# A hybrid decoder block on one core: sums of retention's results by heads, attention's first values split around the exponentials, next weights within the cover steps

## The chip, the core and the metric

The kernel runs on one core of a Trainium2 chip. The core has a matrix engine (TensorE, PE in the profile; its weight loads are PEld), VectorE (DVE), ScalarE (ACT), GpSimd (POOL) and SyncE (SP), which here only issues transfers. Each engine works through its own list of instructions in order, and an instruction waits for what it needs from the others. Sixteen DMA engines move data between the chip's main memory and the on-chip memory, or within main memory; a transfer is issued by SP or by GpSimd, in the order of that engine's list. The metric is the device time of one execution in microseconds (us), lower is better.

## The reference

The block takes 1024 tokens of width 1024 and computes, in float32:

```python
h = modulate(rms_norm(x, g1), sh1, sc1)              # shift and scale from the conditioning vector
parts = split(h @ w_in)                              # retention q, k, v, gate; attention q, k, v of 3 groups; 2 gates
ro = retention(rotary(rq), rotary(rk) / 16, rv)      # 4 heads, chunks of 128 tokens, state 256 x 512
ro = group_norm(ro) * gn_g + gn_b
ret_out = (silu(rg) * ro) @ w_ret_out                # 2048 -> 1024
for g in 3 groups:                                   # 4 heads each, dilation 1, 4, 16
    o[g], lse[g] = dilated_attention(q[g], k[g], v[g], bias[g])
att = sum over g of softmax(lse)[g] * o[g]
merged = sigmoid(gate_a) * ret_out + sigmoid(gate_b) * (att @ w_att_out)
x = x + g1 * (merged @ w_o)
x = x + g2 * (relu(modulate(rms_norm(x)) @ w_ff1) ** 2 @ w_ff2)
out = rms_norm(x, gf)
```

## The kernel before

Every matrix product is made of three passes (`mm3`, lines 201 to 205): each operand is split into a high part, a rounded copy made by ScalarE, and a low part, the rest, made by a subtraction on VectorE. So each weight tile costs a copy on ScalarE and a subtraction on VectorE before TensorE may use it (`split_w`, lines 191 and 192). Large products are cut into 2 by 2 blocks and use seven block products instead of eight, for which sums of blocks are needed.

The work is a list of steps (`Steps`). A step has weight loads, which SP issues into a ring of three raw tiles (line 85), and a body, which writes out instructions. Before the body of an ordinary step runs, the next two steps' weights are split, if raw tiles and split tiles are there. A step marked manual gets a function instead (`ahead`, or the first argument of its body) and calls it where it wants the next step's weights split. The order in which bodies write their instructions is the order on each engine; nothing is reordered later.

The stages, with their places in the profiled execution: the first norm and the attention values (to about 160 us), queries and keys of retention and attention with the weight sums by DMA (to about 560), values of retention, retention (about 660 to 985), attention keys, scores and values for the first pair of heads (to about 1150) and for the second (to about 1296), the output projections, and the MLP.

**Retention.** Four heads of eight chunks. Each chunk (`chunk`) has state matmuls, scores, and between them the projection of retention's gate. GpSimd makes in each chunk the low part j of a later chunk's queries and keys (line 613) and one power for the norm, gr (line 728), which VectorE uses in its next instruction (line 729). In the first four chunks of the following head, `u_final` finishes a head's result, a quarter at a time, and SP stores it to the main-memory tensor y (line 670); the last head is finished in attention's first step.

**Sums of results.** The output projection of retention needs four sums of the blocks of y: t1 = b11 + b12, t3 = b12 + b22, t2 = t1 + b22, t4 = t2 + b21. They are made by DMAs within main memory that GpSimd issues (`result_sums`, `dma_sum`, lines 563 and 564): a copy, then a transfer that adds into its destination, 2 MB each over all four heads, eight in all. They are issued in attention's first step, after the last head's result is stored, each waiting on GpSimd for the one before. Their readers are loads of the output projection, after 1300 us.

**Attention.** For each pair of heads six steps (`att_step`) project keys and compute the scores of the step before. Then come cover steps (`cover_step`): each projects one tile of the merge gates, so that TensorE has work while softmax and the products with the values go on. For the first pair there are four (n = 0 to 3), for the second three, and `gate_step` is its fourth. Their contents:

- n = 0: the scores of the last combination; `scores_end` (maxima, line 1254; exponentials in place with their sums, line 1266), `weights` (the merge weights of the three groups, lines 1336 to 1347, with one exponential on ScalarE at line 1340), `pscale` of group 0 (probabilities times weights, VectorE line 1361 and ScalarE line 1363).
- n = 1: only the gate tile; in its middle `v_split` makes the high (vh, ScalarE, line 1295) and low (vl, VectorE, line 1296) parts of group 0's values.
- n = 2: products of group 0's probabilities with the values (`pv`), woven with the gate matmuls; the split of group 1's values.
- n = 3, or the gate step: products of group 1 (and 2), and `pscale` of group 2 after the fourth k block of the gate matmuls.

In `pv`, TensorE transposes blocks of probabilities (line 1378), ScalarE and VectorE split the transposed block (pth, ptl, lines 1382 and 1383), and TensorE multiplies (lines 1402 to 1404). At the end of a head the result is added up on VectorE (line 1415), which frees the accumulator for the next. The values are loaded by SP (`v_fetch`, line 1289), group 0's in the last of the six steps.

Of the kernel before, what the change touches and what calls it, by code (L numbers as in the profile page):

```python
# [17 lines left out]
P = 128  # L18
# [116 lines left out]
def block_kernel(ctx, tc, io, stop=None, dbg=None):  # L135
# [3 lines left out]
    def fv(t):  # L139
        return t.bitcast(F32)  # L140
# [382 lines left out]

    y_d = dram.tile([P, 4, 8, 512], F32, name="y")
    yt_d = {n: dram.tile([P, 8, 512], F32, name=f"y{n}") for n in ("t1", "t2", "t3", "t4")}
    YB = ("11", "12", "21", "22")

    WN = ("11", "12", "22", "s1", "s2", "s3", "s4")  # L530
# [26 lines left out]
        nc.gpsimd.dma_start(s4, s2)  # L557
        add(s4, src[1, j])

    def dma_sum(out, x, y):  # L560

        flat = lambda t: t.rearrange("p a b -> p (a b)").rearrange("p (a b) -> p a b", b=2048)
        nc.gpsimd.dma_start(flat(out), flat(x))
        nc.gpsimd.dma_start(flat(out), flat(y), accum_op=ALU.add, max_dma_last_dim=8192)
# [6 lines left out]
    def result_sums():  # L571
        b11, b12, b21, b22 = (y_d[:, i] for i in range(4))
        dma_sum(yt_d["t1"], b11, b12)
        dma_sum(yt_d["t3"], b12, b22)
        dma_sum(yt_d["t2"], yt_d["t1"], b22)
        dma_sum(yt_d["t4"], yt_d["t2"], b21)

    hd = {}
# [23 lines left out]
    def flat(ps):  # L602
        return ps.rearrange("p a b -> p (a b)")
# [56 lines left out]
    def u_final(h, es=range(4)):  # L660
        for e in es:
            i = h * 4 + e
            t = hd["on", h][e]
            for hf in range(2):
                neg = 16 if hf == i % 2 else 0
                b = t[:, 512 * hf:512 * hf + 512]
                nc.scalar.activation(b, b, AF.Identity, scale=gnv[0][:, neg + i:neg + i + 1],
                                     bias=gnv[1][:, neg + i:neg + i + 1])
            nc.vector.tensor_mul(t, t, hd["srg", h, e])
            nc.sync.dma_start(y_d[:, 2 * (i % 2):2 * (i % 2) + 2, i // 2], t.rearrange("p (t x) -> p t x", t=2))  # L670

    def chunk(h, c, ahead, w=None):
        p = R["p"]
# [61 lines left out]
            nc.scalar.activation(hd["srg", h, c // 2], flat(hd["rgp"]), AF.Silu)  # L735
        if h > 0 and c < 4:
            u_final(h - 1, (c,))

    def wsplit(ap):
        return ap, split_w  # L740
# [547 lines left out]
            lo = A["l", g, j] = v_tile(pair, g, j, "vl")  # L1288
            nc.sync.dma_start(fv(lo).rearrange("p (a b) -> p a b", a=4), v_rows(pair, g, j))

    def v_split(pair, g):
        for j in range(2):
            lo = A["l", g, j]
            hi = v_tile(pair, g, j, "vh")
            nc.scalar.copy(hi, fv(lo))
            nc.vector.tensor_sub(lo, fv(lo), fv(hi))
            A["v", g, j] = (hi, lo)

    def vblk(g, blk, a, i):
        j, b = (blk % 2, blk // 2) if g == 1 else (blk // 4, blk % 4)  # L1300
# [26 lines left out]
    def weights(pair):  # L1327

        p, st = A["p"], A["st"]
        stn = [st[:, 0], A["stn"][:, 1], A["stn"][:, 2]]  # L1330
        mx = p.tile([P, 8, 2], F32, tag="mx", name=f"mx{pair}")
        wt = p.tile([P, 3, 8, 2], F32, tag="wt", name=f"wt{pair}")
        pr = p.tile([P, 3, 8, 2], F32, tag="pr", name=f"pr{pair}")
        sm = p.tile([P, 8, 2], F32, tag="ssum", name=f"ssum{pair}")
        wg = p.tile([P, 2, 8, 2], F32, tag="wg", name=f"wg{pair}")
        nc.vector.tensor_max(mx, stn[0][:, :, 0:2], stn[1][:, :, 0:2])
        nc.vector.tensor_max(mx, mx, stn[2][:, :, 0:2])
        for g in range(3):
            nc.vector.tensor_sub(wt[:, g], stn[g][:, :, 0:2], mx)
        nc.scalar.activation(wt, wt, AF.Exp)  # L1340
        for g in range(3):
            nc.vector.tensor_mul(pr[:, g], wt[:, g], stn[g][:, :, 2:4])
# [123 lines left out]
    def att_step(pair, i):  # L1466

        g, a = combos[i]

        def body(*args):  # L1470
            ps = ps_mm(f"ak{pair}{i}")
            gen = proj_gen(ps, args[-1])
            if i == len(combos) - 1:
                v_fetch(pair, 0)
            if i > 0:
                last = combos[i - 1]
                weave(gen, NK, scores_gen(pair, *last), len(SB[last[0]]), lag=2)
            elif pair == 0:
                args[0](1, True)
                for _ in range(4):  # L1480
                    next(gen)
                on_T(H - 1, NC - 1)
                drain(gen)
                u_final(H - 1)
                result_sums()
                open_att()
                args[0](3)
            else:

                weave_pv(at(gen, 0, lambda: v_split(0, 2)), NK - 1, 0, 2)  # L1490
            if i == 0:
                A["st"] = A["p"].tile([P, 3, 8, 4], F32, tag="st", name=f"st{pair}")
                bias_load(pair)
            k_split(pair, g, a, ps)
            if i > 0:
                scores_end(pair, *last)
                if last[1] == 1:
                    stats_out(pair, last[0])
        return body

    def cover_step(pair, n):
# [34 lines left out]
    for pair in range(2):  # L1536
# [14 lines left out]
    def gate_step(w):  # L1551
# [72 lines left out]
    def r_x_load(i):  # L1624

        n, c = RSEQ[i]
        b = RPLAN[n][0]
        src = y_d[:, YB.index(b)] if b in YB else yt_d[b]
        for m in range(4):
            Q["x", i, m] = mh(f"rl{i}{m}")  # L1630
            nc.sync.dma_start(fv(Q["x", i, m]), src[:, 4 * c + m])

    def r_x(i, j):

# [818 lines left out]
```

## Time and profile before

| | us |
|---|---|
| median of 3 runs | 2242.24 (2241.17 to 2242.70) |
| the profiled execution | 2241.44 |
| its span, first to last instruction | 2239.7 |
| TensorE busy | 2183.1 (97%) |
| VectorE busy | 1456.5 (65%) |
| ScalarE busy | 908.5 (41%) |
| GpSimd busy | 145.9 (7%) |

The TensorE clock granted was 0.995 of full speed over the span. The times of one engine's rows are its own; a row that says "x3" merges three like instructions in a row. A bracket behind a row gives the engine's idle time before it and what ended it. A wait for several events is put down to the one that came last. The profile's ends of matmuls are modelled: consecutive matmuls overlap, so a matmul's row may be longer than the distance to the next.

### The profile page before, as it was taken

How to read it: one execution, taken by the hardware profiler on the slowest of the kernel's cores; microseconds unless marked ns; L12 is line 12 of the kernel's file. 1: busy time of each engine (PE TensorE's matmuls, PEld its weight loads, DVE VectorE, ACT ScalarE, POOL GpSimd, SP SyncE). 2: the span in 40 equal slices, each digit the busy share in tenths (PEclk: the TensorE clock that was granted, in tenths of full speed). 3: DMA queues.
4: the chain of work that ended last, by engine and by line, in shares of the span. 5: the costliest groups of instructions: out<-in, count | busy, mean ns of one | idle time of the engine just before them, and what ended most of it. 6: DMA issues, size and time to landing. Idle time of an engine off the chain costs nothing.

```text
span 2239.7 us, 27138 instructions
## 1 busy us (share of the span) xinstructions
PE 2183.1 (97%) x10130; PEld 1805.4 (81%) x10130; DVE 1456.5 (65%) x2285; ACT 908.5 (41%) x1665; POOL 145.9 (7%) x168
## 2 busy tenths in 40 slices
PE   7999999999999999999999999999999999999998
PEld 5887888888887888888888788888777777888887
DVE  6527777764548778855555654677866665787845
ACT  4332332223334445544634634524444444533412
POOL 0001110000012122200000000001000000000003
PEclk9999999999999999999999999999999999999999
DMA  9538999634775556559723365654243343745322
GB/s 362 198 142 263 295 286 291 188 113 174 240 272 188 169 182 202 191 171 238 225 73 98 91 225 178 244 182 148 75 151 139 139 155 150 269 144 169 122 85 76
DMA packets 154371, 408.93 MB, mean 183 GB/s; under 512 B 27062, under 2 KB 54973, under 8 KB 149822
## 3 DMA queue, kind: packets, MB, share of 16 engines
q1 hardware_dynamic: 148542, 363.14, 46.4%
q0 software_dynamic: 5696, 44.04, 8.2%
q8 instruction: 80, 1.31, 0.2%
q14 instruction: 53, 0.43, 0.1%
HBM read 316.27 MB, written 156.13 MB: 211 GB/s over the span
## 4 chain that ended last, share of the span: by engine, by line
PE 81%; DVE 9%; ACT 4%; DMA 4%; issue 2%; POOL 0%; SPq 0%; POOLq 0%; DVEq 0%; ACTq 0%
PE qap L201 5%; PE qap L205 5%; PE qap L203 5%; PE av L763 4%; PE rg L203 2%; PE rg L201 2%; PE rg L205 2%; PE fp L201 2%; PE fp L203 2%; PE fp L205 2%; PE ak L201 2%; PE f2a L203 2%; PE f2a L205 2%; PE f2a L201 2%; PE ak L203 2%
## 5 line engine op out<-in xcount | busy, mean ns | idle before, releaser
L201 PE MATMUL qap<-hh,qaw 128*128 128x512 f32 x216 | 85.1, 394 | 4.7 <-DVE qat L285 4.7
L203 PE MATMUL qap<-hl,qaw 128*128 128x512 f32 x216 | 85.0, 393 | 0.0
L205 PE MATMUL qap<-hh,qaw 128*128 128x512 f32 x216 | 85.0, 393 | 0.0
L613 POOL TENSOR_TENSOR j<-qk,j 128x512 fp32r<-128x512 f32 x32 | 43.8, 1369 | 460.0 <-ACT j L612 460.0
L1912 ACT ACTIVATE a<-a 128x512 f32<-128x512 f32 x48 | 30.3, 632 | 84.9 <-DVE a L1911 84.9
L258 DVE TENSOR_TENSOR qaw<-wa,qaw 128x512 fp32r<-128x512 f32 x54 | 37.0, 686 | 36.4 <-ACT qaw L248 36.4
L1266 ACT ACTIVATE P<-P,ng 128x128 f32<-128x128 f32 (+1 forms) x96 | 41.9, 438 | 39.2 <-DVE ng L1263 39.2
L258 DVE TENSOR_TENSOR fw<-w1r,fw 128x512 fp32r<-128x512 f32 x48 | 33.0, 688 | 37.5 <-ACT fw L248 37.5
L1809 POOL TENSOR_TENSOR accnf<-accnf,sqnf 128x256 f32<-128x256 f32 (+1 forms) x18 | 16.6, 921 | 624.3 <-ACT sqnf L1808 624.3
L2096 ACT CAST w2h<-w2s 128x512 fp32r<-128x512 f32 x36 | 22.4, 622 | 79.1 <-DVE w2s L2134 76.1
L201 PEld LDWEIGHTS qap<-hh,qaw 128*128 128x128 f32 x216 | 41.1, 190 | 13.6 <-issue 5.1
L201 PE MATMUL fp<-h2h,fw 128*128 128x512 f32 x128 | 50.0, 390 | 0.0
L203 PE MATMUL fp<-h2l,fw 128*128 128x512 f32 x128 | 49.8, 389 | 0.0
L201 PE MATMUL roa<-rh,rwl 128*128 128x512 f32 x128 | 49.8, 389 | 0.0
L203 PE MATMUL roa<-rl,rwh 128*128 128x512 f32 x128 | 49.8, 389 | 0.0
L205 PE MATMUL roa<-rh,rwh 128*128 128x512 f32 x128 | 49.8, 389 | 0.0
L205 PE MATMUL fp<-h2h,fw 128*128 128x512 f32 x128 | 49.8, 389 | 0.0
L1647 DVE TENSOR_TENSOR rwl<-rwl,rwh 128x1024 fp32r<-128x1024 f32 x25 | 30.2, 1221 | 29.0 <-ACT rwh L1677 29.0
L205 PEld LDWEIGHTS qap<-hh,qaw 128*128 128x128 f32 x216 | 41.1, 190 | 8.7
L203 PEld LDWEIGHTS qap<-hl,qaw 128*128 128x128 f32 x216 | 41.1, 190 | 8.5
L635 ACT COPY sm<-sT 128x128 f32<-128x128 f32 x32 | 8.5, 265 | 94.3 <-PE sT L626 94.3
L1809 POOL TENSOR_TENSOR accn<-accn,sqn 128x512 f32<-128x512 f32 x12 | 15.5, 1294 | 478.4 <-ACT sqn L1808 478.4
(3081 smaller groups left out, 7186.1 us busy)
## 6 DMA issues: line engine op xcount, KB each, us to landing
v<-vd SPq DMA_DIRECT2D x32, 512.0 KB, 5.5
raw<-in_w_ada_dram SPq DMA_DIRECT2D x32, 512.0 KB, 5.0
w1r<-in_w_ff_dram SPq DMA_DIRECT2D x32, 512.0 KB, 5.1
vd<-vo SPq DMA_DIRECT2D x24, 512.0 KB, 6.4
yt<-y POOLq DMA_DIRECT2D x6, 2048.0 KB, 15.3
xsd<-as SPq DMA_DIRECT2D x24, 512.0 KB, 2.7
w2r<-in_w_ff2s_dram SPq DMA_DIRECT2D x24, 512.0 KB, 7.6
em<-in_w_ada_dram SPq DMA_DIRECT2D x16, 512.0 KB, 10.2
```

The source lines that it names most:

```text
L201: nc.tensor.matmul(o, wl, xh, start=first, stop=False, skip_group_check=skip)
L203: nc.tensor.matmul(o, wh, xl, start=False, stop=False, skip_group_check=skip)
L205: nc.tensor.matmul(o, wh, xh, start=False, stop=last, skip_group_check=skip)
L258: nc.vector.tensor_sub(t[:, 512:], src, fv(t[:, :512]))
L613: nc.gpsimd.tensor_sub(t[:, 1], src, fv(t[:, 0]))
L635: nc.scalar.copy(sm, ps[:, :C])
L763: nc.tensor.matmul(av[g][c], x[k][:, c * C:(c + 1) * C], w[j][:, ws], start=k == 0 and (x, j) == parts[0], stop=k == NK - 1 and (x, j) == ...
L1266: nc.scalar.activation(v, v, AF.Exp, bias=ng[:, blk:blk + 1], accum_out=st[:, g, blk, 2 + a:3 + a])
L1647: nc.vector.tensor_sub(lo, fv(lo), fv(hi))
L1809: (nc.vector if f == 7 else nc.gpsimd).tensor_add(G["acc", key], G["acc", key], sq)
L1912: nc.scalar.activation(o, o, AF.Relu)
L2096: nc.scalar.copy(hi, src)
```

## The change

It has three parts.

1. **Sums by heads.** y and the four sum tensors become one tensor per head. A head's eight transfers (four copies, four adds, 512 KB each) are put on a list after the fourth chunk of the following head; each chunk ends with issuing one from the list (`result_sum`). The chunks from the thirteenth on issue one each, 20 in all; the remaining 12, four of the third head and eight of the last, are issued in attention's first step, where the eight large ones were.
2. **First values around the exponentials.** The high parts of group 0's values are made in cover step 0, after the gate tile's matmuls and ahead of `scores_end`; the low parts in `weights`, behind the exponential. Cover step 1 is left with the gate tile alone.
3. **Next weights within the step.** Cover step 3 and the gate step become manual. They split the next step's weights after the fourth k block, just ahead of `pscale` of group 2, instead of the next two steps' weights ahead of everything. The second of these splits is made ahead of the body of the step behind.

TensorE's list of instructions is unchanged.

```diff
-    y_d = dram.tile([P, 4, 8, 512], F32, name="y")
+    y_d = [dram.tile([P, 4, 2, 512], F32, name=f"y{h}") for h in range(H)]
...
+    def sums_of(h):
+        b11, b12, b21, b22 = (y_d[h][:, i] for i in range(4))
+        t1, t2, t3, t4 = (yt_d[n][h] for n in ("t1", "t2", "t3", "t4"))
+        return [(t1, b11, 0), (t1, b12, 1), (t2, t1, 0), (t2, b22, 1), (t4, t2, 0), (t4, b21, 1), (t3, b12, 0),
+                (t3, b22, 1)]
+
+    def result_sum():
+
+        if hd["sums"]:
+            out, x, add = hd["sums"].pop(0)
+            out, x = (t.rearrange("p a b -> p (a b)") for t in (out, x))
+            if add:
+                nc.gpsimd.dma_start(out, x, accum_op=ALU.add, max_dma_last_dim=8192)
+            else:
+                nc.gpsimd.dma_start(out, x)
...
         if h > 0 and c < 4:
             u_final(h - 1, (c,))
+        result_sum()
+        if h > 0 and c == 3:
+            hd["sums"] += sums_of(h - 1)
...
-    def v_split(pair, g):
+    def v_split(pair, g, low=True):
         for j in range(2):
             lo = A["l", g, j]
             hi = v_tile(pair, g, j, "vh")
             nc.scalar.copy(hi, fv(lo))
-            nc.vector.tensor_sub(lo, fv(lo), fv(hi))
             A["v", g, j] = (hi, lo)
+            if low:
+                v_low_part(g, j)
...
         nc.scalar.activation(wt, wt, AF.Exp)
+
+        for j in range(2):
+            v_low_part(0, j)
...
-                result_sums()
+                hd["sums"] += sums_of(H - 1)
+                while hd["sums"]:
+                    result_sum()
...
                 drain(gen)
+                v_split(pair, 0, False)
                 scores_end(pair, *combos[-1])
                 weights(pair)
...
             elif n == 1:
-                drain(at(gen, 4, lambda: v_split(pair, 0)))
+                drain(gen)
...
-                weave_pv(at(gen, 3, lambda: [pscale(2, a) for a in range(2)]), NK - 1, pair, 1)
+
+                gen = at(gen, 3, lambda: (args[0](2), [pscale(2, a) for a in range(2)]))
+                weave_pv(gen, NK - 1, pair, 1)
...
-            steps.add(cover_step(pair, n), more + [wsplit(io["w_gate"][len(COVER[0]) * pair + n])], manual=n == 2)
+            steps.add(cover_step(pair, n), more + [wsplit(io["w_gate"][len(COVER[0]) * pair + n])], manual=n > 1)
...
-        gen = at(gen, 3, lambda: [pscale(2, a) for a in range(2)])
+        gen = at(gen, 3, lambda: (ahead(2), [pscale(2, a) for a in range(2)]))
...
-    steps.add(gate_step, [wsplit(io["w_gate"][len(COVER[0] + COVER[1])])])
+    steps.add(gate_step, [wsplit(io["w_gate"][len(COVER[0] + COVER[1])])], manual=True)
```

More of the change, by code (lines that the diff above doesn't have):

```diff
@@ L522, in etile @@
         return R["p"].tile([P, 1024], dt, tag="E", bufs=12, name=name)
-    y_d = dram.tile([P, 4, 8, 512], F32, name="y")
-    yt_d = {n: dram.tile([P, 8, 512], F32, name=f"y{n}") for n in ("t1", "t2", "t3", "t4")}
+    y_d = [dram.tile([P, 4, 2, 512], F32, name=f"y{h}") for h in range(H)]
+    yt_d = {n: [dram.tile([P, 2, 512], F32, name=f"y{n}{h}") for h in range(H)] for n in ("t1", "t2", "t3", "t4")}
     YB = ("11", "12", "21", "22")
@@ L558, in quarter_sums @@
         add(s4, src[1, j])
[L560 to L564, printed above, removed]
     def gn_signs():
@@ L569, in gn_signs @@
             nc.vector.tensor_scalar_mul(gnv[i][:, 16:], vec[:, v:v + 16], -1.0)
[L571 to L578, printed above, removed]
+    def sums_of(h):
[11 more added lines that the diff above has]
+                nc.gpsimd.dma_start(out, x)
+    hd = {"sums": []}
     NG = H * NC
@@ L669, in u_final @@
             nc.vector.tensor_mul(t, t, hd["srg", h, e])
-            nc.sync.dma_start(y_d[:, 2 * (i % 2):2 * (i % 2) + 2, i // 2], t.rearrange("p (t x) -> p t x", t=2))
+            nc.sync.dma_start(y_d[h][:, 2 * (i % 2):2 * (i % 2) + 2, e // 2], t.rearrange("p (t x) -> p t x", t=2))
     def chunk(h, c, ahead, w=None):
@@ L1295, in v_split, with v_low_part @@
             nc.scalar.copy(hi, fv(lo))
-            nc.vector.tensor_sub(lo, fv(lo), fv(hi))
             A["v", g, j] = (hi, lo)
+            if low:
+                v_low_part(g, j)
+    def v_low_part(g, j):
+        hi, lo = A["v", g, j]
+        nc.vector.tensor_sub(lo, fv(lo), fv(hi))
     def vblk(g, blk, a, i):
@@ L1549, in block_kernel, with gate_step @@
     mh_ctx = ExitStack()
-    def gate_step(w):
+    def gate_step(ahead, w):
         ps = ps_mm("gate9")
         gen = at(proj_gen(ps, w), 2, lambda: v_split(1, 2))
-        gen = at(gen, 3, lambda: [pscale(2, a) for a in range(2)])
+        gen = at(gen, 3, lambda: (ahead(2), [pscale(2, a) for a in range(2)]))
         weave_pv(gen, NK - 1, 1, 1, 2)
@@ L1627, in r_x_load @@
         b = RPLAN[n][0]
-        src = y_d[:, YB.index(b)] if b in YB else yt_d[b]
         for m in range(4):
+            h = 2 * c + m // 2
+            src = y_d[h][:, YB.index(b)] if b in YB else yt_d[b][h]
             Q["x", i, m] = mh(f"rl{i}{m}")
-            nc.sync.dma_start(fv(Q["x", i, m]), src[:, 4 * c + m])
+            nc.sync.dma_start(fv(Q["x", i, m]), src[:, m % 2])
     def r_x(i, j):
```

## The prediction

> **What bounds the kernel now.** I read the page first (busy time by engine), then the busy time by stage, then who waited for whom on TensorE, and last the three engines' rows in order of time around each of these waits.
>
> ```profile
> span 2239.7 us, 27138 instructions
> ## 1 busy us (share of the span) xinstructions
> PE 2183.1 (97%) x10130; PEld 1805.4 (81%) x10130; DVE 1456.5 (65%) x2285; ACT 908.5 (41%) x1665; POOL 145.9 (7%) x168
> ```
>
> TensorE is busy 2183.1 of 2239.7 us. The change leaves its instruction list as it is, so only the idle 56.6 us can shrink, or grow. The next view cuts three stages out: the sums of weights by DMA, the part of retention in which the sums of results would now run, and the stage in which they run today (columns: window, length, then busy us and instructions of PE, PEld, DVE, ACT, POOL, clock, DMA share, GB/s).
>
> ```profile
> 180.00:430.00 250.00, 250.00 (x1097) 206.84 (x1096) 182.59 (x289) 74.14 (x128) 32.02 (x46) 0.99 0.89 273
> 754.00:976.00 222.00, 222.00 (x1081) 184.46 (x1080) 179.61 (x373) 105.73 (x264) 41.91 (x46) 1.00 0.55 180
> 993.00:1091.00 98.00, 96.08 (x498) 81.16 (x497) 52.20 (x84) 48.85 (x130) 6.92 (x8) 1.00 0.98 273
> ```
>
> Retention has no TensorE idle at all (222.00 of 222.00) with the DMA engines 0.55 busy. From 993 to 1091 us the eight large sums fill the DMA engines (0.98), yet TensorE loses only 1.92 us there, most of it in the waits below. Moving the sums therefore gains nothing by itself: nothing waits for them today.
>
> The idle time that the change can reach is in the cover steps. TensorE's waits from 1060 to 1320 us (total, times, longest):
>
> ```profile
> PE pv L1402 <- DVE P L1415: 3.4, 4, 0.9
> PE pv L1403 <- DVE ptl010(0, 0, 0)_9158 L1383: 1.2, 1, 1.2
> PE pv L1403 <- DVE ptl110(0, 0, 0)_10497 L1383: 1.2, 1, 1.2
> PE gate L201 <- ACT g00s L1532: 0.8, 1, 0.8
> PE gate L201 <- ACT g04s L1532: 0.8, 1, 0.8
> PE pv L1402 <- DVE vl L1296: 0.7, 1, 0.7
> PE pv L1402 <- issue: 0.5, 1, 0.5
> ```
>
> About 10 us in all, nearly the same in both pairs of heads. Each stands behind a queue on ScalarE and VectorE. ScalarE's rows for the first pair, then VectorE's, then TensorE's (start, length, line, operation, in brackets the idle time before it):
>
> ```profile
> 1074.18 0.40 ACT L1266 ACTIVATE P<-P,ng 128x128 f32<-128x128 f32 x1 [6.08 <-DVE ng L1263]
> ...
> 1085.24 2.00 ACT L1295 CAST vh<-vl 128x1024 fp32r<-128x1024 f32 x2
> ...
> 1107.42 1.03 ACT L191 CAST raw_8615h<-raw 128x1024 fp32r<-128x1024 f32 x1
> 1108.36 1.05 ACT L191 CAST raw_8724h<-raw 128x1024 fp32r<-128x1024 f32 x1
> ```
>
> ```profile
> 1078.29 0.17 DVE L1342 TENSOR_TENSOR pr<-wt,st 128x16 f32<-128x16 f32 x1 [3.48 <-ACT wt L1340]
> ...
> 1086.52 2.36 DVE L1296 TENSOR_TENSOR vl<-vl,vh 128x1024 fp32r<-128x1024 f32 x2
> ...
> 1109.63 1.22 DVE L192 TENSOR_TENSOR raw_8724l<-raw,raw_8724h 128x1024 fp32r<-128x1024 f32 x1
> ...
> 1118.35 2.01 DVE L1415 TENSOR_TENSOR P<-pv,P 128x1024 f32<-128x1024 f32 x1
> ...
> 1130.00 1.23 DVE L1204 SCALAR_TENSOR_TENSOR ql<-raw,qh 128x1024 fp32r<-128x1024 f32 x1 [2.81 <-ACT qh L1203]
> ```
>
> ```profile
> 1089.53 0.39 PE L1403 MATMUL pv<-ptl000(0, 0, 0)_8945,vh 128*128 128x256 f32 x1 [0.46 <-DVE ptl000(0, 0, 0)_8945 L1383]
> ...
> 1111.37 0.38 PE L1403 MATMUL pv<-ptl010(0, 0, 0)_9158,vh 128*128 128x256 f32 x1 [1.16 <-DVE ptl010(0, 0, 0)_9158 L1383]
> ...
> 1120.51 0.36 PE L1402 MATMUL pv<-pth011(0, 0, 0)_9220,vl 128*128 128x256 f32 x1 [0.77 <-DVE P L1415]
> ```
>
> **The change part by part.** Gains are minus, losses plus, in us of TensorE's path.
>
> *Values split early* (the copies vh before the last exponentials, the subtractions vl between the exponential of the weights and their products). ScalarE has 6.08 us idle ahead of 1074.18; the two copies take 2.00. VectorE has 3.48 idle ahead of 1078.29; the two subtractions take 2.36. Both are covered; without that cover they would delay the weights by up to 4.4. What goes is the same work between 1085.24 and 1088.9, which holds the first transposed block back: its low part, and with it the matmul at 1089.53. Without it ScalarE makes that block's high part about 2 us earlier, VectorE its low part at 1087.4, and TensorE, whose gate matmuls end at about 1088.2, goes on at once: its second matmul starts at 1088.4. That is −1.13. The wait of 0.8 for g00s stays: the table load and the scaling ahead of it are not moved. Once in each pair: −2.26.
>
> *Next weights within the step* (fourth cover step, and the gate step of the second pair). Today two splits, 1107.42 to 1109.4 on ScalarE and 1.22 each on VectorE, precede the first block; its low part ends at 1111.3. Without them the block is ready at 1108.5, before TensorE asks at about 1109.8, and the matmul of 1111.37 starts at 1110.03: −1.34 in each pair, −2.68 in all.
>
> The splits do not vanish. One goes behind the first block of the second head, ahead of the scaling of the third group. VectorE then waits for ScalarE's copy (about 0.4) and spends 1.22 before the scaling and before the accumulation L1415 at 1118.35, for which TensorE already waits 0.77. That wait has no slack, so I charge the delay nearly whole: +1.5 in the first pair. The other split now comes after the step, ahead of the query split at 1130.00. ScalarE gives 0.95 to it (rows at 1107.42 and 1108.36 follow one another at that distance), and what follows, ending in the vl subtraction that TensorE awaits for 0.7, starts where it starts today although TensorE comes 0.95 earlier: +1.1. First pair: −1.13 − 1.34 + 1.5 + 1.1 = +0.1, nothing.
>
> In the second pair the moved split goes into a stretch where VectorE is full until it ends
>
> ```profile
> 1282.23 2.01 DVE L1415 TENSOR_TENSOR P<-pv,P 128x1024 f32<-128x1024 f32 x1
> ```
>
> with TensorE behind it (the "issue" wait of 0.5). It arrives 2.47 earlier, VectorE 2.47 less 1.15 earlier: +1.05. The second split falls behind the last accumulation, where VectorE idles: 0. Second pair: −1.13 − 1.34 + 1.05 = −1.4. No instruction of TensorE moves, and SP issues the same DMAs: one store goes ahead of a query load, one weight load behind three gate loads. These feed work more than 10 us off: 0; bounds −0.5 and +1.
>
> *Sums by heads.* 32 transfers of 512 KB in place of 8 of 2 MB, the same bytes. 20 fall into retention, one after each chunk from the thirteenth on, 12 behind it. GpSimd's rows of one chunk, and what such transfers took from issue to landing where weights are summed today (adds at L551, copies at L555):
>
> ```profile
> 872.89 0.54 POOL L728 TENSOR_TENSOR gr<-gr,ct 128x1 f32<-128x1 f32 x1
> 881.07 1.36 POOL L613 TENSOR_TENSOR j<-qk,j 128x512 fp32r<-128x512 f32 x1 [7.64 <-ACT j L612]
> ```
>
> ```profile
> DMA to landing us min/median/max: 5.3/9.8/19.1
> ```
>
> ```profile
> DMA to landing us min/median/max: 4.7/6.5/8.4
> ```
>
> A sum is queued behind gr and ahead of the next j; each waits on GpSimd for the one before it, issued a chunk (some 9.5 us) earlier. Only a landing later than 9.5 + 7.64 = 17.1 us delays j, and behind j the next gr, for which VectorE waits in every chunk. Median landings are far below: 0. The upper bound is priced as a rival; a gain is excluded, as nothing waits in retention. The DMA load rises, by 20 transfers in some 200 us; while weights were summed, GpSimd issued 46 in 250 (first row of the stages) and TensorE ran 250.00 of 250.00 under a DMA share of 0.89. Those landings were measured with VectorE busy 182.59 of 250. [...]
>
> The 12 sums left start at about 976 and run, in series, six adds and four copies: 6 × 9.8 + 4 × 6.5 = 85, to about 1061. The values of the first group are fetched at
>
> ```profile
> 1063.63 1.16 SPq L1289 DMA_DIRECT2D vl<-vad  x2
> ```
>
> ```profile
> DMA to landing us min/median/max: 5.5/6.5/22.7
> ```
>
> so they land in time for the idle ScalarE before 1074.18 (10.5 us later) unless the tail drags on. [...]
>
> **The sum:** +0.1 − 1.4 + 0 = −1.3. The profiled execution took 2241.44 (span 2239.7), so 2240.1; the median of the three runs shown is 0.8 above it, and I give 2240.5.
>
> **The rivals.**
>
> *All of the gain stays* (the late splits hide in slack that I don't see): −2.26 − 2.68 = −4.9, 2236.5 to 2237.3. For it: VectorE is 65% busy. Against: the waits for L1415 have no slack, and the split stands ahead of it.
>
> *The sums hold up retention; slower.* Adds that land near 19.1 instead of 9.8 pass the point of 17.1. Each then holds j, gr and VectorE by 2.0 plus the issue, 2.7. VectorE is busy 179.61 of 222, so it can't win much back. Ten of the 20 are adds; with half of them late, 5 × 2.7 = 13.5: about 2255; none, if all stay below 17.1. For it: 19.1 did occur. Against: that was with up to three in flight and a DMA share of 0.89, not 0.55.
>
> *The values land late; slower.* If the tail of sums lasts past 1063, ScalarE's copies block the exponentials behind them, since ScalarE runs in order. It decides from a landing of about 8.5 us on (10.5 less the copies' 2.0); at the halfway of 6.5 and 22.7, 14.6, the weights are 6 late: about 2246 to 2247, first pair alone. Against: the tail is estimated to be over, and today's 22.7 is under 2 MB sums.
>
> *It only shifts waits*: both pairs like the first, 2241.5 to 2242.3; part of the forecast's range.
>
> **How the numbers follow.** Forecast with the shifted waits 0.65; all of the gain 0.12; retention held 0.12; late values 0.07; the rest 0.04, slower. A measurement of this kernel tells about 0.2%, 4.5 us, from no change: 2237.8 and 2246.7. Faster than that is two thirds of the second case, 0.08; slower the third, half of the fourth and the rest, 0.20; 0.72 lies between. The low end is all of the gain, 2236.5; the high end takes the late values in and leaves most of the held retention out: 2248.
>
> **What the profile after would show.** Right: no TensorE wait at the first pv of the third and fourth cover steps; vh among the exponentials and vl in the 3.48 us gap; the wait for L1415 in the fourth step grown from 0.77 to about 2.2; TensorE still full in retention, GpSimd's DMA issues right behind gr. Wrong: TensorE or VectorE waits for j or gr after 800 us; exponentials that start after the vh copies wait for a DMA; waits for weights (L192) anywhere in attention.

## The result, and the profile after

The changed kernel takes 2244.78 us (median of 20 runs, 2243.28 to 2250.52) against 2241.80 for the kernel before (20 runs beside it, 2239.07 to 2243.30). The ratio is 1.0019, with a 95% interval of 1.0012 to 1.0025: slower by 3.0 us at the medians, by about 4.3 by the ratio. The forecast was 2240.5, a gain of 1.3. The time lies in the forecast range and inside what was called no change, but the sign is wrong, and the interval leaves no change out.

The profiled execution took 2243.81. The head of its page, and then retention and the stage of the large sums (columns: window, length, busy us and instructions of PE, PEld, DVE, ACT, POOL, clock, DMA share, GB/s):

```profile
span 2242.0 us, 27182 instructions
...
PE 2184.0 (97%) x10130; PEld 1807.0 (81%) x10130; DVE 1456.7 (65%) x2285; ACT 909.0 (41%) x1665; POOL 161.7 (7%) x192
```

```profile
754.00:976.00 222.00, 222.00 (x1080) 184.38 (x1079) 179.36 (x373) 105.67 (x263) 55.43 (x65) 1.00 0.75 225
993.00:1091.00 98.00, 95.22 (x497) 80.84 (x496) 52.18 (x84) 48.22 (x129) 6.20 (x9) 1.00 0.61 169
```

Retention is as full as it was (222.00 of 222.00) with a DMA share of 0.75 instead of 0.55, so the 20 sums in it are free. From 993 to 1091 the DMA engines are far less busy (0.61 for 0.98), and still TensorE is idle longer there: 98.00 − 95.22 = 2.78 for 1.92. TensorE's waits from 1000 to 1320 us show why, and where else (total, times, longest):

```profile
PE pv L1417 <- DVE P L1430: 4.9, 4, 2.3
PE pv L1417 <- DVE vl L1309: 1.8, 1, 1.8
PE sc L203 <- DVE kl L1220: 1.6, 1, 1.6
...
PE pt120(0, 0, 0)_10674 L1393 <- DVE P L1376: 0.7, 1, 0.7
```

The waits for ptl010 and ptl110 (1.2 each) are gone; the wait for L1430 (L1415 before) has grown from 3.4 to 4.9, that for vl from 0.7 to 1.8, and the wait for kl is new. Line numbers are 4 to 20 higher than before.

**The new wait, for kl** (the low part of a step's attention keys). Rows of ScalarE, VectorE and TensorE, and the issues ahead of them, first of the kernel before, then of the changed one:

```profile
992.47 0.35 SPq L85 DMA_DIRECT2D raw<-in_w_ak_dram  x1
992.91 2.89 SPq L1190 DMA_DIRECT2D bias<-biasd  x6
993.40 0.60 POOL L563 DMA_DIRECT2D yt<-y  x1 [17.05 <-DMA y<-on]
996.42 1.05 ACT L191 CAST raw_8152h<-raw 128x1024 fp32r<-128x1024 f32 x1 [2.62 <-DMA raw<-in_w_ak_dram]
1004.41 1.89 DVE L1243 TENSOR_TENSOR P<-sc,bias 128x512 f32<-128x512 f32 x3 [5.69 <-DMA bias<-biasd]
1006.22 1.22 DVE L1213 TENSOR_TENSOR kl<-ak,kh 128x1024 fp32r<-128x1024 f32 x1
1007.49 0.38 PE L203 MATMUL sc<-kl,qh 128*128 128x256 f32 x1
```

```profile
987.50 0.82 POOL L578 DMA_DIRECT2D yt<-y  x1 [4.24 <-DMA yt<-yt]
988.05 0.81 POOL L580 DMA_DIRECT2D yt<-y  x1
992.38 0.35 SPq L85 DMA_DIRECT2D raw<-in_w_ak_dram  x1
992.82 7.08 SPq L1197 DMA_DIRECT2D bias<-biasd  x6
1002.51 1.05 ACT L191 CAST raw_8191h<-raw 128x1024 fp32r<-128x1024 f32 x1 [8.79 <-DMA raw<-in_w_ak_dram]
1006.11 1.89 DVE L1250 TENSOR_TENSOR P<-sc,bias 128x512 f32<-128x512 f32 x3 [1.30 <-DMA bias<-biasd]
1007.92 1.21 DVE L1220 TENSOR_TENSOR kl<-ak,kh 128x1024 fp32r<-128x1024 f32 x1
1009.18 0.38 PE L203 MATMUL sc<-kl,qh 128*128 128x256 f32 x1 [1.64 <-DVE kl L1220]
```

Before, the first large sum waits 17.05 us for y and starts at 993.40, behind SP's weight load. Now the sums of the third head's results are running when attention's first loads are issued. The weights, issued at the same time, are used at 1002.51 instead of 996.42; the six bias loads keep SP 7.08 us instead of 2.89; the biases come 1.7 later; and kl, which was ready exactly when TensorE wanted it (1006.22 + 1.22 = 1007.44, used at 1007.49), is 1.7 late. The last wait ahead of kl is VectorE's for the biases (1.30): the late weights are split by 1003.59 + 1.23 = 1004.82, and alone they would have delayed the row of 1004.41 by some 0.4. The large sums had held up the biases too. The slowest one seen lands 10.5 us after its issue before the change and 13.2 after it, but 4.8 in the kernel below that has no sums beside them (part 1 with gated sums).

**The cover steps.** The rows that answer to those shown of before, in the first pair and, the last two, in the second:

```profile
1069.70 1.99 ACT L1302 CAST vh<-vl 128x1024 fp32r<-128x1024 f32 x2
1076.42 2.36 DVE L1309 TENSOR_TENSOR vl<-vl,vh 128x1024 fp32r<-128x1024 f32 x2
1079.97 0.18 DVE L1357 TENSOR_TENSOR pr<-wt,st 128x16 f32<-128x16 f32 x1 [1.20 <-ACT wt L1352]
1120.84 0.36 PE L1417 MATMUL pv<-pth011(0, 0, 0)_9247,vl 128*128 128x256 f32 x1 [2.35 <-DVE P L1430]
1137.18 0.33 PE L1417 MATMUL pv<-pth020(0, 0, 0)_9393,vl 128*128 128x128 f32 x1 [1.83 <-DVE vl L1309]
1281.88 0.66 PE L1393 MATMUL pt120(0, 0, 0)_10674<-ct,P 128*128 128x128 f32 x4 [0.68 <-DVE P L1376]
1284.11 0.39 PE L1418 MATMUL pv<-ptl111(6, 0, 6)_10665,vh 128*128 128x256 f32 x1 [0.34 <-DVE ptl111(6, 0, 6)_10665 L1398]
```

The copies vh fill ScalarE's idle time, the subtractions vl the gap ahead of pr, which shrinks from 3.48 to 1.20. All of this is as forecast. What is not: after each of the two long waits TensorE runs at half its clock. Busy time by windows of the changed kernel around the wait that ends at 1120.84 and the one that ends at 1137.18 (the clock is the third number from the right):

```profile
1118.50:1121.90 3.40, 1.06 (x8) 1.05 (x9) 2.65 (x3) 0.48 (x1) 0.00 (x0) 1.00 0.23 93
1121.90:1125.30 3.40, 3.40 (x13) 2.82 (x12) 0.00 (x0) 0.48 (x1) 0.00 (x0) 0.50 0.00 0
1125.30:1128.70 3.40, 3.40 (x24) 3.10 (x24) 2.16 (x2) 0.00 (x0) 0.00 (x0) 1.00 0.00 0
...
1135.50:1138.90 3.40, 1.72 (x14) 1.68 (x15) 3.40 (x5) 1.61 (x3) 0.00 (x0) 1.00 0.89 324
1138.90:1142.30 3.40, 3.40 (x12) 2.72 (x11) 0.56 (x1) 0.30 (x1) 0.00 (x0) 0.51 0.68 230
```

In 3.40 us TensorE issues 13 matmuls instead of 24: it is never idle, so no view of waits shows it, and about 1.6 us are lost each time.

**Where the time went, stretch by stretch.** For every matmul, its start in one kernel less its start before; the table gives how much this shift grows in each stretch. The stretches are named by the step in them; their ends on the time scale of the kernel before are 1000, 1012, 1096, 1116, 1130, 1160, 1275, 1290 and 2225 us. All numbers come from TensorE's rows of the profiled executions, us.

| kernel | up to 1000 | kl | first values, pair 1 | first block, pair 1 | L1430 wait | vl wait | both gains, pair 2 | split, pair 2 | rest | sum |
|---|---|---|---|---|---|---|---|---|---|---|
| changed | −0.1 | +1.8 | −1.3 | −1.6 | +3.1 | +2.7 | −2.9 | +1.1 | −0.4 | +2.5 |
| part 1 alone | −0.7 | +2.3 | 0.0 | 0.0 | 0.0 | 0.0 | 0.0 | 0.0 | +1.3 | +2.9 |
| part 2 alone | −0.3 | −0.1 | +6.5 | 0.0 | 0.0 | 0.0 | −1.3 | −0.1 | −0.3 | +4.4 |
| part 3 alone | −1.6 | −0.1 | 0.0 | −1.6 | +3.1 | +2.7 | −1.6 | +1.1 | +0.2 | +2.3 |
| parts 2 and 3 | −1.2 | −0.1 | +5.6 | −1.6 | +3.2 | +1.1 | −2.8 | +1.1 | −0.4 | +4.9 |
| changed, TensorE's waits filled | −0.1 | +5.8 | −1.3 | −1.6 | +1.6 | +1.2 | −2.8 | +1.1 | +3.1 | +7.0 |
| gated sums alone | −1.0 | −0.1 | 0.0 | 0.0 | 0.0 | +1.6 | 0.0 | 0.0 | −0.5 | +0.1 |
| gated, with part 2 | −1.2 | −0.1 | −1.3 | 0.0 | 0.0 | 0.0 | −1.3 | 0.0 | −0.3 | −4.2 |
| gated, all three parts | −0.3 | −0.1 | −1.3 | −1.6 | +1.6 | +2.7 | −2.9 | +1.1 | +1.6 | +0.9 |
| gated, all, filled | 0.0 | −0.1 | −1.3 | −1.6 | +1.6 | +1.2 | −2.8 | +1.1 | +2.7 | +0.8 |
| gated, split behind the accumulation | 0.0 | −0.1 | −1.3 | −1.6 | 0.0 | +1.6 | −2.9 | 0.0 | +0.2 | −4.1 |

The terms are alike from kernel to kernel within 0.1, except where a transfer is late, or where half clock comes in steps of 1.6 (or 3.3). Where in an execution those steps fall varies, as shown below, and they make most of the first and the last column; so the sum of one execution is not the median of its kernel.

### The profile page after: what moved, and what is told of

Same layout as the page of the kernel before. It is cut to its first block, busy times and chain, and to the rows that moved or that the text cites. A ratio compares the mean times of both kernels' runs of the same rounds, so it can differ in the third digit from the quotient of the medians.

```text
span 2242.0 us, 27182 instructions
## 1 busy us (share of the span) xinstructions
PE 2184.0 (97%) x10130; PEld 1807.0 (81%) x10130; DVE 1456.7 (65%) x2285; ACT 909.0 (41%) x1665; POOL 161.7 (7%) x192
## 4 chain that ended last, share of the span: by engine, by line
PE 82%; DVE 8%; DMA 4%; ACT 4%; issue 2%; SPq 0%; POOL 0%; POOLq 0%; DVEq 0%; ACTq 0%
PE qap L201 5%; PE qap L203 5%; PE qap L205 5%; PE av L770 4%; PE rg L203 2%; PE rg L201 2%; PE rg L205 2%; PE fp L201 2%; PE fp L203 2%; PE fp L205 2%; PE f2a L203 2%; PE f2a L205 2%; PE f2a L201 2%; PE ak L201 2%; PE ak L203 2%
```

## The experiments

The theory after the two traces (theory A) had two parts: the tail of the sums collides with attention's first loads (1.8), and idle times of TensorE of about 1.8 us and more cost a half clock behind them (twice 1.6). Its rivals: the sums as a whole cost the time; the moved splits alone do.

### One part at a time

Four kernels: the kernel before with part 1, with part 2 and with part 3, and with parts 2 and 3. Each is the diff shown above, cut to the part.

> The kernel before with part 1 alone (sums by heads). Theory A (the sums cost where their tail meets attention's first loads): retention stays full on TensorE, one new wait of about 1.6 us near 1009 us for kl, median +1.5 to +2 against before (about 2243.5). Rival (sums in retention or the sums as a whole carry the whole loss): +3 or more. Rival (the sums cost nothing, all of the loss is in the cover steps): within 0.5 us of before.

> The kernel before with part 2 alone (first values split early). By the prediction's own step: 1.13 per pair, -2.3 against before (about 2239.5), no wait over 1.8 us and a granted clock of 1.00 from 1060 to 1300. Rival (the gain is taken back by the wait for L1415 within the same step): -1 or nothing.

> The kernel before with part 3 alone (next weights within the step). Theory A (waits of 1.8 us and more cost a clock drop of about 1.6 each on top): waits of about 2.3 and 1.8 in the first pair with the clock at 0.5 for some 3 us behind each; the waits alone come to +1.3 in the first pair and -0.3 in the second, +1.0, and with two drops +4.1 (2246). Rival (waits alone, the clock is no cost): +1.0. Rival (part 3 gains as forecast, -1.34 per pair): -0.3 or better.

> The changed kernel without part 1: the sums are made as before. Theory A: no wait for kl near 1009, both clock drops still there; 1.5 to 2 under the changed kernel (about 2243, +1.5 against before). Rival (the sums are the whole loss): back to the forecast of the two parts, -1.3. Rival (the sums cost nothing): as the changed kernel, +3.

Against 2242.30 for the kernel before in the same series (medians, ratio and interval): part 1 2244.93, 1.0011 [1.0002, 1.0020]; part 2 2244.76, 1.0014 [1.0005, 1.0023]; part 3 2244.26, 1.0011 [1.0002, 1.0020]; parts 2 and 3 2249.38, 1.0034 [1.0021, 1.0047]. All four are slower, by 2.0 to 7.1 us at the medians, and parts 2 and 3 (5 runs) lose more than with part 1 added (the changed kernel, +3.0 in its own series): the parts are not independent.

Part 1 has the wait for kl (2.16 in this execution) and nothing else up to 1290, as theory A has it; its median, +2.6, lies between theory A's +2 and the rival's +3, and the gated sums below decide. Part 3 has both long waits and both half clocks: −1.6 + 3.1 + 2.7 = +4.2 in the first pair and −0.5 in the second, +3.7 where +4.1 was expected (its execution had 1.6 less before 1000, by a half-clock stretch that was shorter). At the median part 3 costs only 2.0, between theory A's 4.1 and the 1.0 of waits alone, so not every execution need have both half clocks: in that of parts 2 and 3 the wait for vl (1.81) had none behind it. Part 2 fell the other way: not −2.3 but +2.5. Its rows (issue of the values' loads, the copies of them, and TensorE's first transposition behind) show what happens when the large sums stay where they were:

```profile
1063.63 1.07 SPq L1289 DMA_DIRECT2D vl<-vad  x2
...
1076.58 1.05 ACT L1295 CAST vh<-vl 128x1024 fp32r<-128x1024 f32 x1 [8.88 <-DMA vl<-vad]
...
1078.89 1.05 ACT L1295 CAST vh<-vl 128x1024 fp32r<-128x1024 f32 x1 [1.26 <-DMA vl<-vad]
...
1085.63 0.69 PE L1386 MATMUL pt000(0, 0, 0)_8939<-ct,P 128*128 128x128 f32 x4 [2.82 <-DVE P L1369]
```

The values are used 13 us after their issue; ScalarE, in order, holds the exponentials behind the copies; TensorE waits 2.82 and then, for the scaled gate, 3.78, and runs at half clock for 6.8 us. That is the rival "the values land late" of the prediction, which the 2 MB sums bring about and the smaller, earlier ones of part 1 avoid. So part 2 is no gain while large sums run beside its loads, and parts 2 and 3 without part 1 are the worst of all, not 1.5 to 2 better than the changed kernel: theory A had left that out.

### Is it the clock? Useless work in the waits

The changed kernel, with the transpositions of one block ahead of each of the two long waits made four times (21 extra ones). The waits end when VectorE is done, as they did, but TensorE is idle for less:

```diff
+        if pair == 0 and (g, a, bank) in ((1, 1, PT[1][2]), (2, 1, PT[2][0])):
+            for i, (q, half, k) in enumerate(bank * 3):
+                nc.tensor.transpose(pt[:, i % len(bank) * 128:(i % len(bank) + 1) * 128],
+                                    pslice(g, t, q)[0][:, half * 128:half * 128 + 128], ident)
```

> The changed kernel with useless work added to TensorE: the three transposes of one block ahead of the 2.35 us wait, and the four ahead of the 1.83 us wait, are made four times in a row (21 extra transposes, some 1.1 us each place), so that the waits end where they ended but TensorE is idle for about 1.3 and 0.8 us only. Theory A (the length of the idle time sets the clock): granted clock 1.00 behind both, and the kernel is 2.5 to 3.2 us faster than the changed one (about 2241.5) although it does more. Rival (the clock drop has another cause, or costs nothing): as the changed kernel or slower by up to 2.

TensorE's two waits, and the clock around the first (windows up to and behind its end):

```profile
1124.94 0.36 PE L1421 MATMUL pv<-pth011(0, 0, 0)_9247,vl 128*128 128x256 f32 x1 [1.41 <-DVE P L1434]
1139.74 0.33 PE L1421 MATMUL pv<-pth020(0, 0, 0)_9402,vl 128*128 128x128 f32 x1 [0.53 <-DVE vl L1309]
```

```profile
1122.00:1125.00 3.00, 1.59 (x14) 1.32 (x12) 3.00 (x6) 0.48 (x1) 0.00 (x0) 1.00 0.39 153
1125.00:1129.00 4.00, 4.00 (x29) 3.69 (x30) 0.82 (x2) 0.48 (x1) 0.00 (x0) 1.00 0.00 0
```

Both half clocks are gone, and the two stretches cost 1.65 + 1.17 instead of 3.13 + 2.72: 3.0 us less, with 21 instructions more. The median, 2243.84, is 2.2 under that of the next kernel, whose TensorE waits are those of the changed one, in the same series. It is still 1.8 above the kernel before (2242.05 in this series; 1.0010 [1.0001, 1.0019]), so the expected 2241.5 was not reached; the profiled execution itself had a wait of 2.87 for kl with 6.8 us of half clock behind it (+5.8 together). The wait for kl varies from execution to execution, 1.64 to 2.87 in the four profiles that have it, and can bring a half clock of its own; the changed kernel's runs spread wider than those before, up to 2250.52.

### Moving the tail of the sums

First a miss. The 12 sums left after retention were issued in the third to fifth steps of attention instead of the first:

```diff
-                while hd["sums"]:
-                    result_sum()
...
+            if pair == 0 and i >= 2:
+                for _ in range(4):
+                    result_sum()
```

> The changed kernel, but the 12 sums left after retention are issued four at a time in the third to fifth steps of attention, behind the first loads of bias and key weights. Theory A (these sums hold up the bias and weight loads from 990 to 1003 us): no wait for kl near 1009, about 1.6 us faster than the changed kernel (2243); the values' load at 1063 may land later, which would show as a wait of exponentials. Rival (the wait is the price of the shorter, denser retention or of the stores of y by heads): the wait of 1.6 stays.

2246.01 against 2242.05, 1.0021 [1.0012, 1.0031]; the wait for kl was there (1.82, a shift of +1.97). It does not speak for the rival: GpSimd has nothing else to do in attention, so its list ran ahead and issued the first sums at the times of the changed kernel (982.60 and 987.33 for 982.75 and 987.50; the last at 1044.27 for 1039.60). A place in the program is no time.

So they were given something to wait for: a one-column addition on GpSimd that reads the second pair's bias, ahead of the sums.

```diff
 def bias_load(pair):
...
+        if pair == 1:
+            late = A["p"].tile([P, 1], F32, tag="late", name="late")
+            nc.gpsimd.tensor_add(late, bt[:, 1279:1280], bt[:, 1279:1280])
+            while hd["sums"]:
+                result_sum()
```

> Part 1 alone, but the 12 sums left after retention wait on GpSimd for the second pair's bias (a one-column addition that reads it), so that they run after about 1130 us. Theory A (retention's sums are free; the tail's collision with the loads at 980 to 1005 is the whole price of part 1): no wait for kl near 1009, same as before within 0.6 us. Rival (the tail costs wherever it stands): +1.5 or more, with a wait in the second pair's steps.

> The same with part 2 added (first values split early). Theory A: without any sums beside the values' load at 1063 the copies don't wait, 1.3 per pair is gained as in the changed kernel, -2.6 against before (2239.5). Rival (the values land late for another reason than the sums): the exponentials wait for the copies again and it is slower than before by 2 or more, as with part 2 alone.

> The changed kernel with the 12 sums gated in this way: all three parts, without the collision. Theory A: 1.8 under the changed kernel, and still both clock drops behind the 2.35 and 1.83 waits: +1 against before (2243). Rival (no collision, no clock drops): -1.3, the forecast.

Against 2241.43 in this series: part 1 gated 2241.45, 0.9999 [0.9991, 1.0008]; with part 2 2238.08, 0.9988 [0.9979, 0.9997]; with all three 2242.27, 1.0006 [0.9998, 1.0015]. No wait for kl in any of them, and the gains of part 2 are there in both pairs. So part 1's whole price is the tail beside attention's first loads. With all three parts both long waits remain (2.32 and 1.83), and they show that the length of a wait alone does not set the half clock:

```profile
1118.78 0.36 PE L1422 MATMUL pv<-pth011(0, 0, 0)_9235,vl 128*128 128x256 f32 x1 [2.32 <-DVE P L1435]
```

```profile
1114.20:1117.60 3.40, 2.27 (x14) 1.72 (x12) 3.40 (x13) 1.50 (x5) 0.00 (x0) 1.00 0.49 154
1117.60:1121.00 3.40, 2.22 (x13) 1.94 (x14) 1.50 (x2) 0.00 (x0) 0.00 (x0) 1.00 0.00 0
1121.00:1124.40 3.40, 3.40 (x27) 3.22 (x26) 1.48 (x2) 0.48 (x1) 0.00 (x0) 1.00 0.00 0
...
1131.30:1134.70 3.40, 1.57 (x12) 1.13 (x12) 3.40 (x5) 2.20 (x4) 0.00 (x0) 1.00 0.93 335
1134.70:1138.10 3.40, 3.40 (x12) 2.71 (x12) 1.15 (x2) 0.00 (x0) 0.00 (x0) 0.50 0.80 279
```

The wait of 2.32 fell across two windows, 1.13 and 1.18 idle, and no half clock followed; the shorter one of 1.83 lay in one window and was followed by one. Over the four kernels of the table that have both long waits unfilled (changed, part 3, parts 2 and 3, this one) six of the eight were followed by one. The windows shown are, within 0.1, those of the clock record itself: within one execution the half-clock stretches begin on one grid of 3.41 us, which lies elsewhere in another execution (the starts before and after stand in the last section).

### All causes taken away

The gated kernel with all three parts, and the fill as above:

> All three parts, the 12 sums gated on the second pair's bias, and the extra transposes of the fill in the first pair, so that TensorE's idle time ahead of the two long waits is 1.2 and 0.5 us instead of 2.3 and 1.8. Theory A (collision and clock drops are all that lies between forecast and result): the forecast's own sum comes out, -1.3 to -2 against before, about 2240; 1.5 to 3 under the same kernel without the fill. Rival (the moved splits cost more than forecast by themselves): as the same kernel without the fill, +0.8.

2240.50 against 2242.30, 0.9992 [0.9983, 1.0001]: 1.8 faster at the medians, though the interval just touches no change; without the fill the same kernel was 0.8 slower than the kernel before in its series. The profiled execution's shift at 1290 us, from the gains and the shifted waits, is −1.9 (its +2.7 in the last column is a half clock of 6.8 us at 1901 us, behind a wait that the kernel before has too). With the two causes gone the forecast's own sum comes out, as far as the medians can tell.

### A better version

Two kernels put the split elsewhere: the next weights are still split within the step, but after the sixth and seventh k block of the gate's matmuls, behind the accumulation L1415 instead of ahead of it.

```diff
-                gen = at(gen, 3, lambda: (args[0](2), [pscale(2, a) for a in range(2)]))
+                gen = at(gen, 3, lambda: [pscale(2, a) for a in range(2)])
+                gen = at(gen, 5, lambda: args[0](2))
+                gen = at(gen, 6, lambda: args[0](1, True, 2))        # the step after next
...
-        gen = at(gen, 3, lambda: (ahead(2), [pscale(2, a) for a in range(2)]))
+        gen = at(gen, 3, lambda: [pscale(2, a) for a in range(2)])
+        gen = at(gen, 5, lambda: ahead(2))
```

Without part 1 (and beside it the kernel with part 2 and the gate step's share of part 3 alone):

> The kernel before with part 2 and another part 3: the next weights are split within the fourth cover step and the gate step too, but after the sixth and seventh k block of the gate matmuls, behind the accumulation of the first head, so that no split stands ahead of an accumulation that TensorE awaits. Theory A: the waits at the first block go (-1.34 per pair), the wait for the accumulation stays near 0.8 to 1.2, no clock drop: -3.5 to -4.9 against before (2237 to 2238.3). Rival (the wait for the accumulation grows anyway because TensorE comes earlier): -2.3, as with part 2 alone.

> The kernel before with part 2 and, of part 3, the gate step alone (second pair). Theory A: the first pair gains 1.13 and has no long wait, the second 1.4: -2.5 against before (about 2239.3), granted clock 1.00 throughout. Rival (the second pair gains nothing, its split only shifts the wait): -1.1 to -1.5.

Against 2242.05 they came to 2245.11, 1.0008 [0.9999, 1.0017], and 2245.75, 1.0017 [1.0009, 1.0026]. Both are misses, as the expectations had left out what part 2 alone had shown: both lose 6.5 us at the late values, like part 2 alone, and gain what was expected elsewhere (in the second pair −2.87 and 0.00, and −2.83 and +1.12).

With the gated sums by heads:

> The gated sums, part 2, and the next weights split within the step behind the accumulation (after the sixth and seventh k block). Theory A: gains of 1.3 and 1.5 per pair stay and no wait grows: -5.6 on TensorE's path against before, less one clock drop of 1.6 that a pile of short waits may set off by chance: 2236.5 to 2238. Rival (what is gained is taken back by chance drops): -2 or less.

2236.76 against 2241.43, 0.9977 [0.9968, 0.9986]: faster than the kernel before by 4.7 at the medians, as expected. TensorE's waits from 1000 to 1320 us, all of the length they had before, without those of the first blocks:

```profile
PE pv L1422 <- DVE P L1435: 3.3, 4, 0.9
...
PE pv L1422 <- DVE vl L1314: 0.7, 1, 0.7
PE pv L1422 <- issue: 0.5, 1, 0.5
```

Last, whether part 1 is needed in it: the eight large sums as before, all gated on the second pair's bias.

> The best version without part 1: the eight large sums of the kernel before, all of them gated on the second pair's bias, with part 2 and the splits behind the accumulation. Theory A (the sums cost only beside attention's first loads; that 20 of them run in retention buys nothing): as the best version with sums by heads, -4.2 to -4.9 against before, unless the sums last past the values' load of the second pair at about 1222 us. Rival (the sums must be spread over retention for the values to come in time): slower than the best version by 2 or more, with a wait of exponentials in the second pair.

2245.69 against 2242.30, 1.0020 [1.0011, 1.0029]. The first pair gains all that the best version gains (no wait for kl, −1.3 and −1.6), with no sum made in retention at all. But the large sums run on (the last is issued at 1217.17), and loads of the second pair come late beside them, first a gate weight (issued at 1194.53, used at 1216.60), then the values:

```profile
1216.60 1.05 ACT L191 CAST raw_9842h<-raw 128x1024 fp32r<-128x1024 f32 x1 [6.55 <-DMA raw<-in_w_gate_dram]
1219.65 0.36 PE L201 MATMUL sc<-kh,ql 128*128 128x256 f32 x1 [2.43 <-DVE P L1247]
1222.42 0.58 PE L203 MATMUL sc<-kl,qh 128*128 128x256 f32 x1 [2.41 <-DVE kl L1217]
...
1235.39 1.05 ACT L1299 CAST vh<-vl 128x1024 fp32r<-128x1024 f32 x1 [5.78 <-DMA vl<-vad]
...
1248.05 0.74 PE L201 MATMUL gate<-hh,raw_9944l 128*128 128x512 f32 x2 [2.39 <-ACT g04s L1548]
```

The gate weight costs most: two waits of 2.4 and 6.8 us of half clock, together a shift of +7.4. The late values add 1.6. So sums in retention buy no time by themselves; they leave fewer sums to place, and what counts is that none runs beside a load that attention is about to use.

## Why the prediction was wrong, step by step

*Values split early, −2.26:* right in mechanism and place; measured −1.3 in each pair, −2.6 (column "first values", and the gated kernel with part 2).

*Next weights within the step, −2.68 at the first blocks:* right; −1.6 in each pair, −3.1.

*The moved splits, +1.5, +1.1 and +1.05:* right to 0.1. The wait for L1415 grew from 0.77 to 2.35, the wait for vl from 0.7 to 1.83, and the second pair lost 1.1, as two waits of 0.68 and 0.34 instead of one.

*The sums in retention, 0:* right; the rival "the sums hold up retention" fell. TensorE is full there (222.00 of 222.00), and part 1 with a gated tail is equal to before, 0.9999 [0.9991, 1.0008].

*The 12 sums left, part of the sums by heads at 0:* the first step that failed. The prediction said that nothing waits for the sums, and asked how late the tail ends (1061, for the values at 1063; in the trace its last transfer is issued at 1039.60), not what it meets when it starts. Attention's first loads, at 992 us, are in none of its terms; its bounds of −0.5 and +1 are for the order of SP's loads in the cover steps. The rows of before show that these loads had no slack: VectorE is idle for 5.69 on the biases, and kl is ready 0.05 ahead of TensorE. Measured: +1.8 in this execution, with a wait of 1.64, and waits of 1.82 to 2.87 in three other kernels with the tail in that place. One of the prediction's own signs of being wrong was there: VectorE waits 7.84 for the weights of L192 at 1003.59, for 1.65 before.

*What is missing altogether, and the second step that failed:* the price of a long wait behind its end. The prediction charged +1.5 and +1.1 for the grown waits as if TensorE resumed at full speed. The trace of before had the warning; TensorE's wait for onm ends at 681.51, and the windows around it show the clock:

```profile
681.51 0.44 PE L631 MATMUL kT<-ct,qk 128*128 128x128 f32 x2 [2.65 <-DVE onm L731]
```

```profile
678.60:682.10 3.50, 0.70 (x5) 0.32 (x4) 2.70 (x8) 0.27 (x1) 0.58 (x1) 1.00 0.82 295
682.10:685.50 3.40, 3.39 (x8) 2.75 (x9) 3.33 (x7) 0.00 (x0) 0.00 (x0) 0.51 0.20 36
```

A step that turns a wait of 0.77 into 2.3 should have been charged 1.5 + 1.6, and the one to 1.8 at least a part of it: +3.1 in this execution.

The budget at 1290 us, measured: −2.6 − 3.1 + 1.6 + 1.1 + 1.1 = −1.9 (forecast −1.3), + 1.8 for kl, + 3.1 for two half clocks, −0.1 before 1000: +2.9. The trace has +2.90 there. That the time lies within the range is luck: the high end, 2248, stood for late values. Of the rivals, *all of the gain stays* was rightly put low: it takes another place for the splits, as the best version shows. *The values land late* is a real mechanism, and decides where the large sums run at 1063; in the changed kernel itself it does not occur, since the tail is over by then.

What stays open: what each of the loads at 992 us would cost alone. The trace puts the last wait on the biases, but taking the tail away mends weights and biases at once, and no run delays the weights alone. Open too is why, of waits of like length, one has a half clock behind it and another none (for vl, 1.83 in the changed kernel and 1.81 in parts 2 and 3).

## What to carry to other kernels

When background transfers are moved, look at what they meet at the beginning of their new place, not only at when they end: a load whose user is idle on it already has no slack at all (here the biases, for which VectorE was idle for 5.69 us), and a place in an idle engine's list does not fix a time (moved from attention's first step to its third, a sum was issued at 982.60 us for 982.75), only a wait does. And price a TensorE wait by what follows it: here short waits that were merged into one of 2.35 us cost as much again in granted clock, 1.5 of wait and 1.6 behind it, and 21 transpositions of no use, put into the two long waits, saved 3.0 us on these two stretches. Put a split that must be moved behind the row that another engine awaits, not ahead of it.

## What the runs showed of the hardware

In the clock records before and after, which begin at 23 us, the half-clock stretches of TensorE up to 2230 us are 3.41 or 6.83 us long, and within an execution they lie on one grid of 3.41 us: they begin at 176.98, 682.15 and 1644.71 us before and at 176.38, 681.55, 1121.87, 1138.94 and 1647.53 after, each time whole multiples of 3.413 us apart, and the two grids lie 0.60 us apart. All eight begin behind a window of the grid in which TensorE was idle for 1.65 us or more (3.41, 2.80 and 3.16 before; 3.30, 2.64, 2.35, 1.65 and 3.16 after); at the 1.65, behind the wait of 1.83 for vl, TensorE was busy for 1.76 of the window's 3.41. At full clock, the longest idle sums of a window with no half clock behind it are 1.52 before and 1.64 after, the latter the wait for kl.

The other runs show that this is no sharp threshold. The wait of 1.81 in parts 2 and 3, that of 2.16 for kl in part 1 alone and that of 2.32 in the gated kernel with all three parts, which fell across two windows, had no half clock behind them. And the wait of 0.9 for the last accumulation of a pair, which stands among short matmuls of 128 columns and is in the kernel before too (0.88 and 0.92), without a half clock, was followed by one in the best version (0.89, first pair), in its form without part 1 (0.90, first pair) and in the gated one with all three parts (0.91, second pair). In the table, the gated sums alone have a +1.6 in the same stretch as the best version. One such stretch costs 1.6 us: the shift in the stretch of the vl wait is +2.7 with it (changed) and +1.1 without it (parts 2 and 3). These steps are most of the first and last columns of the table, and they are why one execution's sum says less than its stretches.
